# Row factors from squares of the turned input, x in four half slabs, and block sums on GpSimd

## The chip, the cores and the metric

The kernel runs on one core of a Trainium2 chip. The metric is the device time of one execution in microseconds. The times given are the median of three runs and, where a profile is read, the one execution that the hardware profiler recorded.

## The reference, cut to what matters

Two layers of a sandwich-normalised mixer over 512 positions of width 2048, with 256 memory tokens:

```python
def rmsnorm(x, g):
    y = x * lax.rsqrt(jnp.mean(x * x, axis=-1, keepdims=True) + EPS)
    return y * g

for l in range(2):
    h = rmsnorm(x, pre_norm_g[l])                 # x: 512 x 2048
    z = h @ w_in[l]                               # 2048 x 4928
    q_lat, kv_lat, k_pe, gb, gc, xin, q_mem, gate = split_cols(z)
    a_out = mla_attention(...)                    # 8 heads, low-rank q and kv, rotary part
    c_out = short_gated_conv(gb, gc, xin, conv_w[l])
    mem_n = rmsnorm(mem, mem_norm_g[l])           # mem: 256 x 2048
    m_out = memory_attention(q_mem, mem_n, w_mk[l], w_mv[l])   # 4 heads over 256 tokens
    y = concatenate([a_out, c_out, m_out]) * silu(gate)
    x = x + rmsnorm(y @ w_o[l], post_norm_g[l])
```

Everything is float32. The kernel gets x and mem also in turned form (the model width on the partitions), laid out by the host.

## The kernel before, in words

Every float32 product is made as three products of a high and a low part (`mm3`: high by high, low by high or high by low, L253 to L255). ScalarE casts a tile to its high part and VectorE subtracts to get the low part. For weights this is `Program.prep` (L177 and L178) on tiles of 128 x 1024, read by a ring of eight raw tiles (`wr`), with three high (`wh`) and three low (`wl`) tiles. For operands on the left it is `split_to` (L258, L259).

The two large projections use a Strassen form: seven products P1 to P7 of half blocks. Their left operands are A11, A12, A22 and the block sums S1 to S4 (`LEFT`, L357). The weight sums are made on the way in, with accumulating DMAs from the GpSimd queue (`more`, L154). `HEAD`, `STEADY` and others (L400) give the order of the passes. A pass has four steps c = 0 to 3, and a step is 12 matmuls of 512 columns.

`Program.run` goes through a list of steps. For each it issues loads ahead on SP's queue, prepares weights two units ahead, emits the step's work, and then lets put-off work (`pr.defer`) go out as far as the step's `room` covers its cost. `pr.until` and `pr.settle` force it. TensorE, SP and GpSimd keep the order in which the program emits. ScalarE and VectorE keep it up to `first.close`; behind that a scheduler orders them.

Layer 0 starts with the memory products: eight pairs of steps, `keys(kp)` (24 matmuls of 256 columns into four PSUM banks) and `values(kp)` (12 of 512 into two). mem's turned blocks are scaled by a gain column and split (L183, L184). Beside them stand the row factors of x and mem. `row_factors` (L564) loads rows of 128 x 2048, squares them on ScalarE with a running sum (L573), and takes the power -1/2 on GpSimd (L575, L576). `factor_row` (L579) spreads a factor column, turns it on TensorE (L588) and copies it out (L589), so that it can multiply turned data. `turned_load` and `turned_scale` (L591, L595) load x turned in blocks of 128 tokens and multiply by gain and factor row (L598). `left_half` splits A11 and A12.

After the memory steps the kernel runs P1 and P2 of group 0, P1 and P2 of group 1, and then P5 of group 0, the first pass to need a block sum. Tokens 256 to 511 are loaded and scaled during P1 and P2 of group 0 and P1 of group 1. `right_half` and `combine` (L383 to L398) put off the block sums, all on VectorE (L386), with their splits, once per block of 128 tokens:

```python
put_off(nc.vector.tensor_tensor, a22, a22, a21, op=ALU.subtract)
split("S1", a22)
put_off(nc.vector.scalar_tensor_tensor, a22, a22, -1.0, a11, op0=ALU.mult, op1=ALU.subtract)
split("S2", a22)
```

At the end of `values(7)` and `keys(7)` the memory keys and values are scaled, split and written to DRAM (`Kmd`, `Vmd`, L735), to be read back for the attention. Layer 1 does the memory steps again with its own gain and weights, between the transposes of the new x (`transpose_rows`, L601).

Of the kernel before, what the change touches and what calls it, by code (L numbers as in the profile page):

```python
# [12 lines left out]
P = 128  # L13
# [50 lines left out]
class Unit:  # L64
# [6 lines left out]
    def __init__(self, key, loads=None, more=None, sums=(), then=(), place=None, alloc=None, gain=None):  # L71
        self.key = key
        self.loads = loads or {}
        self.more = more
        self.sums, self.then = sums, then
        self.place = place
        self.alloc = alloc
        self.gain = gain


class Program:
# [36 lines left out]
    def run(self):  # L118
# [39 lines left out]
        def prep(upto):  # L158
            while at["prep"] < min(upto, len(seq)):
# [16 lines left out]
                if u.gain is None:  # L176
                    nc.scalar.copy(hi[:, :n], src)  # L177
                    nc.vector.tensor_tensor(lo[:, :n], src, hi[:, :n].bitcast(F32), op=ALU.subtract)  # L178
                else:
                    gains = u.gain()  # L180
                    for k, g in enumerate(gains):
                        h = slice(k * (n // len(gains)), (k + 1) * (n // len(gains)))
                        nc.scalar.activation(hi[:, h], src[:, h], AF.Copy, scale=g)  # L183
                        nc.vector.scalar_tensor_tensor(lo[:, h], src[:, h], g, hi[:, h].bitcast(F32),  # L184
                                                       op0=ALU.mult, op1=ALU.subtract)
                for a, b in u.then:
# [22 lines left out]
def encoder(tc, x, xt, mem, memt, positions, columns, w_in, q_norm_g, w_uq, kv_norm_g, w_ukv,  # L209
# [62 lines left out]
    def setup():  # L272
        ident = scrap("ident", P)
        make_identity(nc, ident)
        identr = const.tile([P, P], F32R, name="identr")
        nc.vector.tensor_copy(identr, ident)
        mhalf = const.tile([P, 4], F32, name="mhalf")
# [105 lines left out]
    def combine(left, p, a11, a12, a21, a22):  # L383
# [14 lines left out]
        split("S3", a21)  # L398

# [164 lines left out]
    def row_factors(key, src, t, dst):  # L564

        def load():
            G[key, t] = slab("rows")
            nc.sync.dma_start(G[key, t], src[t * P:(t + 1) * P, :])

        def factor():  # L570
            rows = G.pop((key, t))
            ssq = small()
            nc.scalar.activation(rows, rows, AF.Square, accum_out=ssq)  # L573
            ms = small(1, "ms")
            nc.gpsimd.tensor_scalar(ms, ssq, 1.0 / D, EPS, op0=ALU.mult, op1=ALU.add)  # L575
            nc.gpsimd.tensor_tensor(dst[:, t:t + 1], ms, G["mhalf"][:, :1], op=ALU.pow)  # L576
        return load, factor

    def factor_row(name, ts):  # L579

        src = G[name]
        dst = scrap("row", len(ts) * P)
        G[name + "_row"] = dst.rearrange("p (t c) -> p t c", c=P)
        ps = bank("rps")
        for k, t in enumerate(ts):
            wide = scrap("wide", P)
            nc.vector.tensor_copy(wide, src[:, t:t + 1].broadcast_to([P, P]))
            nc.tensor.transpose(ps[:, k * P:(k + 1) * P], wide, G["ident"])  # L588
        nc.vector.tensor_copy(dst, ps[:, :len(ts) * P])  # L589

    def turned_load(t):  # L591
        G[f"hT{t}"] = slab("hT").rearrange("p (k c) -> p k c", c=P)
        nc.sync.dma_start(G[f"hT{t}"].rearrange("p k c -> p (k c)"), xt[t])

    def turned_scale(t, h):  # L595
        hT, r = G[f"hT{t}"], G["rx_row"][:, t % 2, :]
        for k in range(8 * h, 8 * h + 8):
            nc.vector.scalar_tensor_tensor(hT[:, k, :], hT[:, k, :], G["g1_0"][:, k:k + 1], r,  # L598
                                           op0=ALU.mult, op1=ALU.mult)
# [30 lines left out]
    def projection(l):  # L630
# [33 lines left out]
        def own_lat():  # L664
# [7 lines left out]
            group(L, (l, 0), 512, block((O_GC, O_XI), 512), slot_of("gc", "xi"), HEAD, fin_u, by_two=l == 0),  # L672
# [12 lines left out]
    def mem_steps(l):  # L685

        def unit(name, w, kp):
            return Unit((name, l, kp), {(name, l, kp): [w[kp * 256:(kp + 1) * 256, :].rearrange("(a p) c -> p a c", p=P)]})

        def turned(q):  # L690
            def place():
                if q % 2 == 0:
                    G.setdefault("mT", []).append((slab("mH", F32R), slab("mL", F32R)))
                return tuple(t[:, (q % 2) * 1024:(q % 2 + 1) * 1024] for t in G["mT"][q // 2])
            return Unit(("mT", l, q), {("mT", l, q): [memt[:, 4 * q:4 * q + 4, :]]}, alloc=place,
                        gain=lambda: [G[f"gm_{l}"][:, 4 * q + a:4 * q + a + 1] for a in range(4)])

        def keys(kp):
            def f(*ops):
# [5 lines left out]
                for i in range(4):  # L705
                    for j in range(2):
                        mm3(G["mk"][i][:, :MT], (kh[:, j, i * P:(i + 1) * P], kl[:, j, i * P:(i + 1) * P]),
                            mem_kt(2 * kp + j), kp == 0 and j == 0, kp == 7 and j == 1)
                if kp == 7:
                    km = G["Km"] = slab("Km", F32R).rearrange("p (s i c) -> p s i c", s=2, i=4)  # L710
                    for i in range(4):
                        ks = scrap("ks", MT)
                        nc.vector.tensor_tensor(ks, G["mk"][i][:, :MT], G["rm_row"].rearrange("p t c -> p (t c)"), op=ALU.mult)
                        split_to(km[:, 0, i, :], km[:, 1, i, :], ks)
            return f

        def values(kp):
            def f(wv):
# [5 lines left out]
                if kp < 7:  # L724
                    return
                vm = G["Vm"] = slab("Vm", F32R).rearrange("p (s t c) -> p s t c", s=2, t=2)
                for t in range(2):
                    r = G["rm"][:, t:t + 1]
                    nc.scalar.activation(vm[:, 0, t, :], G["mv"][t], AF.Copy, scale=r)
                    nc.vector.scalar_tensor_tensor(vm[:, 1, t, :], G["mv"][t], r, vm[:, 0, t, :].bitcast(F32),  # L730
                                                   op0=ALU.mult, op1=ALU.subtract)
                G.pop("mT")
                for n in ("Km", "Vm"):
                    d = G[n + "d"] = dram.tile([P, D], F32, name=f"{n}d{l}")
                    nc.gpsimd.dma_start(d, G.pop(n).rearrange("p a b c -> p (a b c)").bitcast(F32))  # L735
            return f
        return [s for kp in range(8) for s in ((keys(kp), [turned(kp // 2)] * (kp % 2 == 0) + [unit("mk", w_mk[l], kp)], 0.8),
                                               (values(kp), [unit("mv", w_mv[l], kp)], 0.8))]

# [320 lines left out]
    def mixer(l, C, gates, pair2, tail):  # L1060
# [13 lines left out]
        for pair in range(4):  # L1074
# [3 lines left out]
            if pair == 2:  # L1078
                nxt.update(pair2)
            for k, v in nxt.items():  # L1080
# [133 lines left out]
    def warm(n):  # L1214

        ps = bank("warm")
        for k in range(n):
            nc.tensor.transpose(ps[:, (k % 4) * P:(k % 4 + 1) * P], G["ident"], G["ident"])
# [21 lines left out]
    add(pr.begin_loads(5))  # L1240
    add(lambda: warm(30))
    G["src"], G["dst"] = x[0], None
    for l in range(depth):
        G["left"] = L = Left(True)
# [5 lines left out]
        turn = [lambda l=l, t=t: transpose_rows(l, t, G[f"hs{t}"]) for t in range(NT)]  # L1250
        ms = mem_steps(l)
        if l == 0:
            add(use)
            G.update(rx=const.tile([P, NT], F32, name="rx"), rm=const.tile([P, 2], F32, name="rm"))
            xr = [row_factors("x", x[0], t, G["rx"]) for t in range(NT)]
            mr = [row_factors("mem", mem[0], t, G["rm"]) for t in range(2)]
            scale = [[lambda t=t, h=h: turned_scale(t, h) for h in range(2)] for t in range(NT)]
            load = [lambda t=t: turned_load(t) for t in range(NT)]
            left = [[lambda t=t, h=h: left_half(t, (h,)) for h in range(2)] for t in range(2)]
# [149 lines left out]
```

## Time and profile before

| | |
|---|---|
| median of 3 runs | 1521.41 us (1520.81 to 1522.31) |
| profiled execution | 1524.05 us |
| its span, first to last instruction | 1522.3 us |
| mean granted TensorE clock | 0.989 |
| TensorE busy | 1484.2 us (98%) |
| VectorE (DVE) busy | 1095.7 us (72%) |
| ScalarE (ACT) busy | 864.1 us (57%) |
| GpSimd (POOL) busy | 256.4 us (17%), most of it DMA issues |

How to read the profile: a row of an order of time has start, duration, engine, line of the kernel, operation, tile written and tiles read, and in brackets the idle time in front and what ended it. A row of a group has the count, then busy time and mean duration, then idle time in front and what ended it. A row of waits has who waited for whom, the total in us, how often, and the longest. A row of a stretch has the busy time of PE, PEld, DVE, ACT and POOL with instruction counts, then the granted clock, the busy share of the DMA engines and GB/s. PE is TensorE's matmul, PEld its weight load. "Landing" is the end of a DMA.

### The profile page before, as it was taken

The numbers are of one execution on the slowest core, as the hardware profiler recorded it, in microseconds if no ns is written. First come the engines' busy times: TensorE is split into PE (matmuls) and PEld (weight loads), VectorE is DVE, ScalarE is ACT, GpSimd is POOL, SyncE is SP. The second block draws the span as 40 slices with busy tenths as digits, with TensorE's granted clock in tenths as the row PEclk, the third lists the DMA queues.
The fourth block names the chain that finished last, engine by engine and source line by source line (L and its number), as shares of the span: only waits on it lengthen the run. The fifth ranks groups of instructions, "written<-read, shape, count | busy, mean of one in ns | idle before, by whom it ended". The sixth has DMA issues, their size and how long they took to land.

```text
span 1522.3 us, 20025 instructions
## 1 busy us (share of the span) xinstructions
PE 1484.2 (98%) x7494; PEld 1273.7 (84%) x7494; DVE 1095.7 (72%) x1503; ACT 864.1 (57%) x1312; POOL 256.4 (17%) x249
## 2 busy tenths in 40 slices
PE   8897999999999999999999999999999999999997
PEld 8776888899888888887888888888998888888886
DVE  5888867656766768778798856776576586698687
ACT  5554443445557768654687533444454587686443
POOL 0022221212310000140220233020313000003211
PEclk9997999999999999999999999999999999999999
DMA  9996997879891111495887999797979521027945
GB/s 371 343 295 117 239 212 189 171 171 223 190 242 53 56 42 49 112 183 182 242 284 222 245 216 231 192 184 174 182 204 220 177 69 44 28 84 137 249 124 181
DMA packets 143746, 271.39 MB, mean 178 GB/s; under 512 B 17312, under 2 KB 40096, under 8 KB 140320
## 3 DMA queue, kind: packets, MB, share of 16 engines
q0 software_dynamic: 51968, 113.00, 38.9%
q1 hardware_dynamic: 91536, 157.06, 31.1%
q8 instruction: 59, 0.97, 0.3%
q14 instruction: 39, 0.32, 0.1%
q10 hardware_dynamic: 144, 0.05, 0.0%
HBM read 257.49 MB, written 12.58 MB: 177 GB/s over the span
## 4 chain that ended last, share of the span: by engine, by line
PE 83%; DVE 5%; issue 3%; ACT 3%; DMA 2%; POOL 2%; POOLq 0%; DVEq 0%; SPq 0%; ACTq 0%
PE P L254 20%; PE P L255 20%; PE P L253 20%; PE ptp L1000 2%; POOL wr L137 2%; PE tps L751 2%; DVE wl L178 2%; DMA wr<-in_w_o_dram 1%; PE o L254 1%; PE o L255 1%; PE o L253 1%; PE sc L253 1%; PE sc L254 1%; PE sc L255 1%; PE sc L980 1%
## 5 line engine op out<-in xcount | busy, mean ns | idle before, releaser
L178 DVE TENSOR_TENSOR wl<-wr,wh 128x1024 fp32r<-128x1024 f32 (+1 forms) x432 | 515.4, 1198 | 294.5 <-ACT wh L177 285.7
L177 ACT CAST wh<-wr 128x1024 fp32r<-128x1024 f32 (+1 forms) x432 | 444.1, 1032 | 481.3 <-PE P L255 383.6
L253 PE MATMUL P<-wh,S 128*128 128x512 f32 (+1 forms) x896 | 346.9, 387 | 9.0 <-ACT S L258 8.6
L255 PE MATMUL P<-wh,S 128*128 128x512 f32 (+1 forms) x896 | 345.1, 385 | 2.9 <-DVE S L259 2.8
L254 PE MATMUL P<-wl,S 128*128 128x512 f32 (+1 forms) x896 | 345.3, 385 | 1.4 <-DVE wl L178 1.4
L253 PE MATMUL P<-wh,A 128*128 128x512 f32 (+1 forms) x656 | 252.6, 385 | 0.0
L254 PE MATMUL P<-wl,A 128*128 128x512 f32 (+1 forms) x656 | 251.8, 384 | 0.8 <-DVE wl L178 0.8
L255 PE MATMUL P<-wh,A 128*128 128x512 f32 (+1 forms) x656 | 251.4, 383 | 0.0
L137 POOL DMA_DIRECT2D wr<-in_w_in_dram x136 | 164.1, 1207 | 461.3 <-DVE wl L178 279.1
L253 PEld LDWEIGHTS P<-wh,S 128*128 128x128 f32 x896 | 169.0, 189 | 40.2 <-ACT S L258 9.7
L255 PEld LDWEIGHTS P<-wh,S 128*128 128x128 f32 x896 | 169.0, 189 | 34.3 <-DVE S L259 4.0
L254 PEld LDWEIGHTS P<-wl,S 128*128 128x128 f32 x896 | 169.1, 189 | 32.3 <-DVE wl L178 2.4
L254 PEld LDWEIGHTS P<-wl,A 128*128 128x128 f32 x656 | 123.2, 188 | 22.6 <-DVE wl L178 1.2
L255 PEld LDWEIGHTS P<-wh,A 128*128 128x128 f32 x656 | 123.1, 188 | 22.2
L253 PEld LDWEIGHTS P<-wh,A 128*128 128x128 f32 x656 | 123.1, 188 | 21.8 <-ACT og L489 0.2
L137 POOL DMA_DIRECT2D wr<-in_w_o_dram x40 | 48.6, 1214 | 545.9 <-DVE wl L178 530.7
L986 ACT ACTIVATE P<-sc,nm 128x512 f32<-128x512 f32 (+1 forms) x96 | 59.9, 624 | 31.2 <-DVE nm L983 31.2
L989 ACT ACTIVATE P<-P,rec 128x512 f32<-128x512 f32 (+1 forms) x96 | 63.2, 661 | 6.6 <-DVE rec L988 6.6
L983 DVE TENSOR_REDUCE nm<-sc 128x1 f32<-128x512 f32 (+1 forms) x96 | 57.2, 596 | 10.5 <-PE sc L981 6.1
L259 DVE TENSOR_TENSOR PT<-ptp,PT 128x512 fp32r<-128x512 f32 (+1 forms) x96 | 54.9, 595 | 10.0 <-ACT PT L258 9.6
L258 ACT CAST PT<-ptp 128x512 fp32r<-128x512 f32 (+1 forms) x96 | 46.4, 522 | 6.3 <-DVE S L259 3.2
L1000 PE MATMUL ptp<-identr,P 128*128 128x128 f32 x320 | 46.4, 274 | 0.7 <-ACT P L986 0.7
(274 smaller groups left out, 2150.1 us busy)
## 6 DMA issues: line engine op xcount, KB each, us to landing
wr<-in_w_in_dram SPq DMA_DIRECT2D x128, 512.0 KB, 5.2
wr<-in_w_in_dram POOLq DMA_DIRECT2D x112, 512.0 KB, 7.3
wr<-in_w_o_dram SPq DMA_DIRECT2D x48, 512.0 KB, 3.9
wr<-in_w_o_dram POOLq DMA_DIRECT2D x40, 512.0 KB, 7.4
wr<-in_w_in_dram SPq DMA_DIRECT2D x32, 416.0 KB, 3.4
wr<-in_w_in_dram POOLq DMA_DIRECT2D x24, 416.0 KB, 6.0
wr<-in_w_mk_dram SPq DMA_DIRECT2D x16, 512.0 KB, 6.8
wr<-in_w_mv_dram SPq DMA_DIRECT2D x16, 512.0 KB, 6.6
```

Of the source, the lines that this page charges most:

```text
L137: engine.dma_start(dst, src, **kw)
L177: nc.scalar.copy(hi[:, :n], src)
L178: nc.vector.tensor_tensor(lo[:, :n], src, hi[:, :n].bitcast(F32), op=ALU.subtract)
L253: nc.tensor.matmul(ps, ah, bh, start=first, stop=False, **kw)
L254: nc.tensor.matmul(ps, ah, bl, start=False, stop=False, **kw)
L255: nc.tensor.matmul(ps, al, bh, start=False, stop=last, **kw)
L258: nc.scalar.copy(hi, src)
L259: nc.vector.tensor_tensor(lo, src, hi.bitcast(F32), op=ALU.subtract)
L983: nc.vector.tensor_reduce(nmax, ps, axis=AX.X, op=ALU.max, negate=True)
L986: nc.scalar.activation(pt, ps, AF.Exp, bias=nmax, accum_out=tot)
L989: nc.scalar.activation(pt, pt, AF.Copy, scale=rec)
L1000: nc.tensor.transpose(ps[:, k * P:(k + 1) * P], pt[:, k * P:(k + 1) * P], G["ident"])
```

## The change

x comes only turned, in four slabs `X[h][g]` (256 tokens by half the width). Its squares (ScalarE, one instruction of 2048 columns a slab) are folded by GpSimd to 256 columns; the sum over partitions is made by a product with a tile of ones, which leaves the factors as a column. mem's squares and their sums are made by GpSimd from the raw tiles that carry mem to the split. The first gain multiplies X on ScalarE (`turned_gain`), the factor row on VectorE (`turned_scale`, 1024 columns). In layer 0 the left operands are now kept by halves of the width. The block sums are made by GpSimd (`combine_turned`); S2 takes its sign in the split. rm is applied to the memory values and keys behind P1's first steps, from PSUM, and its row goes to DRAM for layer 1. mem's turned blocks of layer 1 are scaled and split during layer 0's second pair of attention heads, written to DRAM (`mTd`) and read back. mem's units are half as large in layer 0. The warm-up products at the start read a tile of ones, 44 instead of 30.

```diff
-                    nc.scalar.copy(hi[:, :n], src)
-                    nc.vector.tensor_tensor(lo[:, :n], src, hi[:, :n].bitcast(F32), op=ALU.subtract)
+                    for k in range(u.parts):
+                        h = slice(k * n // u.parts, (k + 1) * n // u.parts)
+                        nc.scalar.copy(hi[:, h], src[:, h])
+                        nc.vector.tensor_tensor(lo[:, h], src[:, h], hi[:, h].bitcast(F32), op=ALU.subtract)
...
+                if u.beside:
+                    u.beside(src)
...
+    def combine_turned(left, x):
+        u = slab("sums").rearrange("p (a k c) -> p a k c", a=2, k=4)
...
+        def pool_op(o, a, b, op):
+            pr.defer(0.0, lambda: nc.gpsimd.tensor_tensor(o, a, b, op=op))
+        for p in two:
+            a11, a12, a21, a22 = views(p)
+            pool_op(u[:, p], a22, a21, ALU.subtract)
+        for p in two:
+            split("S1", p, u[:, p])
+        for p in two:
+            pool_op(u[:, p], u[:, p], views(p)[0], ALU.add)
+        for p in two:
+            pr.defer(1.2, lambda p=p: negated("S2", p, u[:, p]))
+        for p in two:
+            pool_op(views(p)[1], views(p)[1], u[:, p], ALU.subtract)
+        for p in two:
+            split("S4", p, views(p)[1])
+        for p in two:
+            pool_op(views(p)[2], views(p)[0], views(p)[2], ALU.subtract)
+        for p in two:
+            split("S3", p, views(p)[2])
+        for p in two:
+            split("A22", p, views(p)[3])
...
-    def row_factors(key, src, t, dst):
...
+    def turned_squares(h, g):
+        sq = slab("sq")
+        nc.scalar.activation(sq, G["X"][h][g].rearrange("p k c -> p (k c)"), AF.Square)
+        add_up(sq, 2048)
+        if g:
+            first = G["sq", h]
+            nc.gpsimd.tensor_tensor(first[:, :256], first[:, :256], sq[:, :256], op=ALU.add)
+        else:
+            G["sq", h] = sq
+    def add_up(t, n):
+        while n > 256:
+            n //= 2
+            nc.gpsimd.tensor_tensor(t[:, :n], t[:, :n], t[:, n:2 * n], op=ALU.add)
+    def mem_squares(kp):
+        def f(src):
...
+            acc, new = t[:, :512], t[:, 512:1024]
+            nc.gpsimd.tensor_tensor(new if kp else acc, src, src, op=ALU.mult)
+            if kp:
+                nc.gpsimd.tensor_tensor(acc, acc, new, op=ALU.add)
+            if kp == 7:
+                add_up(t, 512)
+        return f
+    def factor_split(h):
+        red = scrap("red", dt=F32R)
+        split_to(red[:, :256], red[:, 256:], G.pop(("sq", h))[:, :256])
+        G["red", h] = red
+    def factor_columns(h, ps, dst):
+        red = G.pop(("red", h))
+        for t in range(2):
+            for i in range(2):
+                nc.tensor.matmul(ps[:, t * P:(t + 1) * P], red[:, i * 256 + t * P:i * 256 + (t + 1) * P], G["onesr"],
+                                 start=i == 0, stop=i == 1)
+        ms = small(NT, "ssq4")[:, :2]
+        nc.vector.tensor_scalar(ms, ps[:, :256].rearrange("p (t c) -> p t c", c=P)[:, :, 0], 1.0 / D, EPS,
+                                op0=ALU.mult, op1=ALU.add)
+        nc.gpsimd.tensor_tensor(dst, ms, G["mhalf"][:, :2], op=ALU.pow)
...
+    def turned_gain(h, g, a):
+        X = G["X"][h][g]
+        for k in range(4 * a, 4 * a + 4):
+            nc.scalar.activation(X[:, k, :], X[:, k, :], AF.Copy, scale=G["g1_0"][:, 8 * g + k:8 * g + k + 1])
+    def turned_scale(h, g, p):
+        X = G["X"][h][g][:, 4 * p:4 * p + 4, :]
+        r = G[f"rx{h}"].rearrange("p (o c) -> p o c", o=1).broadcast_to([P, 4, 256])
+        nc.vector.tensor_tensor(X, X, r, op=ALU.mult)
...
+            if pair == 1 and l + 1 < depth:
+                for k, s in enumerate(mem_turned_steps(l + 1)):
+                    nxt.setdefault(2 * k + 1, []).append(s)
...
             beside = {
-                0: [xr[0][0]], 1: [xr[1][0]], 2: [xr[0][1], load[0]], 4: [xr[1][1], load[1]],
...
+                1: [lambda: turned_load(1, 0)], 2: [squares(0, 0)], 3: [lambda: turned_load(1, 1)],
+                4: [squares(0, 1)], 5: [gain(0, 0, 0)], 6: [gain(0, 0, 1)],
+                7: [lambda: factor_split(0), columns_of(0)], 8: [row_of(0)], 9: [gain(0, 1, 0), squares(1, 0)],
+                10: [scaled(0, 0, 0)], 11: [left_part(0, 0, 0), squares(1, 1)], 12: [scaled(0, 0, 1)],
+                13: [left_part(0, 0, 1), gain(0, 1, 1)], 14: [scaled(0, 1, 0), lambda: factor_split(1), columns_of(1)],
+                15: [left_part(0, 1, 0), row_of(1), lambda: factor_split("m")],
             }
...
+            put(a[:1])
+            add(lambda: factor_columns("m", G["mk"][0][:, MT:], G["rm"]))
+            add(scaled(0, 1, 1))
+            add(left_part(0, 1, 1))
+            put(a[1:2])
+            add(lambda: factor_row("rm_row", G["mk"][1][:, MT:], G["rm"]))
+            add(lambda: values_out(0))
...
+            put(a[2:3])
+            add(lambda: keys_out(0))
+            put(a[3:])
+            add(first.close)
+            for g in range(2):
+                for k in range(2):
+                    add(lambda g=g, k=k: pr.defer(0.0, gain(1, 1 - g, k)))
+            for g in (1, 0):
+                for k in range(2):
+                    add(lambda g=g, k=k: pr.defer(1.2, scaled(1, g, k)))
+            add(lambda: pr.defer(0.0, lambda: combine_turned(G["left"], G["X"])))
```

More of the change, by code (lines that the diff above doesn't have):

```diff
@@ L64, with __init__ @@
 class Unit:
-    def __init__(self, key, loads=None, more=None, sums=(), then=(), place=None, alloc=None, gain=None):
+    def __init__(self, key, loads=None, more=None, sums=(), then=(), place=None, alloc=None, gain=None, parts=1,
+                 beside=None):
         self.key = key
@@ L579, in factor_row @@
[L579 to L593, printed above, removed]
@@ L732, in f @@
[L732 to L735, printed above, removed]
+                if kp == 7:
+                    G.pop("mT")
             return f
-        return [s for kp in range(8) for s in ((keys(kp), [turned(kp // 2)] * (kp % 2 == 0) + [unit("mk", w_mk[l], kp)], 0.8),
+        return [s for kp in range(8) for s in ((keys(kp), [turned(kp)] * (l == 0) + [unit("mk", w_mk[l], kp)], 0.8),
@@ L740, in mem_fetch, with mem_reload @@
+    def mem_reload(h):
+        two = slab("mH", F32R), slab("mL", F32R)
+        for i in range(2):
+            nc.gpsimd.dma_start(two[i], G["mTd"][2 * h + i])
+        G.setdefault("mT", []).append(two)
     def mem_fetch():
@@ L1271, in encoder @@
                     add(f)
-            add(first.close)
         else:
```

191 lines of the change are left out of this document (117 added, 74 removed).

## The prediction, made before the changed kernel ran

> **What bounds the kernel now.** I read the page's engine shares first, then the list of what TensorE (PE) waits for, then PE's order of time around those waits, and last the order of time of VectorE (DVE) and GpSimd (POOL).
>
> ```profile
> PE 1484.2 (98%) x7494; PEld 1273.7 (84%) x7494; DVE 1095.7 (72%) x1503; ACT 864.1 (57%) x1312; POOL 256.4 (17%) x249
> ```
> ```profile
> PE P L253 <- ACT S L258: 8.6, 2, 8.4
> PE mk L255 <- DVE wl L178: 3.3, 4, 1.2
> PE rps L588 <- DVE wide L587: 2.9, 1, 2.9
> PE P L255 <- DVE S L259: 2.8, 1, 2.8
> ```
> ```profile
> 100.00:120.00 20.00, 12.68 (x50) 9.31 (x48) 19.96 (x29) 9.87 (x10) 4.76 (x4) 0.83 1.07 254
> ```
>
> PE is busy 98% of the span, so the time can only come from its 38 us of idleness and from slow clock. The list of waits (total us, times, longest) names the block sums first; its longest entries lie before 130 us, as PE's order of time below shows. In the stretch from 100 to 120 us the columns are PE, PEld, DVE, ACT, POOL busy, then granted clock: while PE stands a third of the time and the clock falls to 0.83, DVE is busy 19.96 of 20 us. That is the block sums S1 to S4 of layer 0, all made by DVE just as P5 needs them. PE's order of time gives the places:
>
> ```profile
> 14.95 0.40 PE L253 MATMUL mv<-wh,mH 128*128 128x512 f32 x1
> ...
> 20.57 0.40 PE L253 MATMUL mv<-wh,mH 128*128 128x512 f32 x1
> ...
> 64.86 0.39 PE L253 MATMUL P<-wh,A 128*128 128x512 f32 x1
> 65.09 0.39 PE L254 MATMUL P<-wl,A 128*128 128x512 f32 x1
> ...
> 110.03 0.50 PE L253 MATMUL P<-wh,S 128*128 128x512 f32 x1 [0.16 <-ACT S L258]
> ...
> 124.02 0.79 PE L253 MATMUL P<-wh,S 128*128 128x512 f32 x1 [8.40 <-ACT S L258]
> ...
> 126.36 0.63 PE L254 MATMUL P<-wl,S 128*128 128x512 f32 x1
> 126.79 0.63 PE L255 MATMUL P<-wh,S 128*128 128x512 f32 x1
> ```
>
> A pair of memory steps takes 20.57 - 14.95 = 5.62 us, so eight pairs take 45. A 512-wide matmul takes 0.23 us at full clock (64.86 to 65.09) and 0.43 behind a long stall (126.36 to 126.79). P1 begins at 64.86, P5 at 110.03. P5 loses 0.16 + 2.78 + 8.40 = 11.3 us of idleness and about 20 slow matmuls of 0.2, 4 us: 15.3 together. Without those, its start would be worth 110.0 + 15.3 = **125.3**. The same point in the changed kernel decides the case; I work out two times, to P1 and from P1 to P5.
>
> **The prices.** DVE's and ACT's groups in the first 70 us (busy, mean ns), then ACT's first row, which waits for mem, and three of DVE's weight splits in a row:
>
> ```profile
> L177 ACT CAST wh<-wr 128x1024 fp32r<-128x1024 f32 x19 | 19.3, 1042 | 10.0 <-PE mk L254 6.2 <-PE mv L255 3.7
> L573 ACT ACTIVATE rows<-rows 128x2048 f32<-128x2048 f32 x4 | 7.7, 1913 | 2.8 <-DMA rows<-in_x_dram 2.8
> L183 ACT ACTIVATE mH<-wr,cols 128x256 fp32r<-128x256 f32 x16 | 6.8, 497 | 0.0
> L184 DVE SCALAR_TENSOR_TENSOR mL<-wr,cols,mH 128x256 fp32r<-128x256 f32 x16 | 6.7, 480 | 5.7 <-ACT mH L183 5.7
> ```
> ```profile
> 5.45 1.28 ACT L183 ACT_TABLE_LOAD   x1 [5.45 <-DMA wr<-in_memt_dram]
> ```
> ```profile
> 9.42 3.50 DVE L178 TENSOR_TENSOR wl<-wr,wh 128x1024 fp32r<-128x1024 f32 x3 [0.45 <-ACT wh L177]
> ```
>
> So DVE does 1024 columns in 3.50 / 3 = 1.17 us. GpSimd has no large sum in this trace. Its nearest rows are small:
>
> ```profile
> 0.72 0.20 POOL masks.py:197 MEMSET ident<- 128x128 f32 x1 [0.29 <-POOLq L1391]
> 1.00 0.29 POOL masks.py:199 TENSOR_SCALAR_AFFINE_SELECT ident<-ident 128x128 f32<-128x128 f32 x1
> 1.25 0.10 POOL L278 MEMSET mhalf<- 128x4 f32 x1
> ```
>
> The fill of 128 columns costs 0.10 us over the smallest one, 0.8 ns a column; one that also reads a tile costs 0.19 over it, 1.5 ns. A second input should add what the first did, 0.7: **2.2 ns** a column as an estimate, with 1.5 as the low bound. That is 2.35 us for 1024 columns, 1.23 for 512, 0.66 for 256.
>
> **Do GpSimd and DVE run side by side?** A DVE row, then two GpSimd rows, of which the second starts inside it, and GpSimd's group of such rows:
>
> ```profile
> 786.87 1.28 DVE L1183 SCALAR_TENSOR_TENSOR xr<-og,r,xr 128x1024 f32<-128x1024 f32 x1
> ```
> ```profile
> 771.10 0.55 POOL L265 TENSOR_TENSOR r<-ms,mhalf 128x1 f32<-128x1 f32 x1 [5.11 <-DVE ms L263]
> ...
> 787.13 1.44 POOL L265 TENSOR_TENSOR r<-ms,mhalf 128x1 f32<-128x1 f32 x1 [2.91 <-DVE ms L263]
> ```
> ```profile
> L265 POOL TENSOR_TENSOR r<-ms,mhalf 128x1 f32<-128x1 f32 x12 | 11.3, 944 | 52.7 <-DVE ms L263 32.1 <-DVE tot L1123 16.6 <-ACT wh L177 3.9
> ```
>
> The same one-column power takes 0.55 us at 771, but 1.44 when it starts inside a DVE instruction with two SBUF inputs. It ends at 788.57, 0.4 us after that instruction's end at 788.15: it has stood for nearly all of it. The group's mean of 944 ns says that this is common. So GpSimd does not read while DVE streams two inputs. Whether DVE waits in turn for a long GpSimd sum no row shows, since these powers read one column. I take it that it does: one way is seen, and a shared path explains it both ways.
>
> The Trainium skill, "SBUF — State Buffer", section "Who interferes with whom", states that rule: a DVE instruction with two SBUF inputs and a GpSimd instruction that reads SBUF exclude each other, and the second waits for all of the first. The trace agrees for GpSimd as the one that waits. By the rule the time is that of the sum in line below; if only what the rows show held, it would be that of the sum side by side.
>
> **The change up to P1.** GpSimd now squares and sums mem (a product and a sum of 512 columns per pair of blocks) and adds up the squares of x, in program order, and PE needs the second pair of row factors before the last values step. Up to there GpSimd has 13 instructions of 512 (16.0 us), four folds 1024 + 512 + 256 (17.0) and two sums of 256 (1.3): 34.3. DVE has 17 weight splits (19.9), 16 mem splits (6.7), five products with the factor row or splits of x (5.9): 32.5, all with two SBUF inputs. If they exclude each other, that is 67 us in line. It starts when the first mem piece lands; half as large as now, it comes before 5.45. I take 4.5. So 71.5, then the last values step, 2.7, and a row copy: **P1 at 75**, 10 us late. Side by side, ACT would set the time: 17 casts (17.3), mem scalings 6.8, squares of x 7.7, 32 gains of 256 columns (13.6 at the mem scaling's price), two casts of x: 47.5, against PE's 45. From 4.5, with the factor's path and the last step behind, that is P1 at 56.5.
>
> Queued behind a late sum: ACT's split of the factor sums and with it ACT's next weight casts; on SP the w_mv loads, since a raw tile is now returned by GpSimd too. What goes away hides nothing: 6 MB of row loads and six row squares, and the 2.9 us wait for rm's row (`rps`). A smaller first piece, its weights split in two halves and an earlier table load bring the first matmul forward; that is inside both P1 times, which start from ACT and DVE.
>
> **From P1 to P5.** New in both cases is rm's row inside P1: its transposes stand on PE after two steps (24 matmuls, 5.5 us), but on DVE the copy that feeds them stands behind eight two-input instructions (five products with the factor row, a split of x, two weight splits), 9.4 us, and a few small ones, 1.0. PE waits 4.9 us, and by the slow rows above some eight matmuls at 0.2 are lost, 1.6. Sixteen steps of twelve matmuls are 43.7 us; with this, **P5 at P1 + 50** if nothing else ends later.
>
> The block sums are eight GpSimd instructions of 1024, behind Km's write in the GpSimd queue, which waits for Km:
>
> ```profile
> 59.43 0.42 DVE L713 TENSOR_TENSOR ks<-mk,row 128x256 f32<-128x256 f32 x1
> ...
> 64.01 0.43 DVE L259 TENSOR_TENSOR Km<-ks,Km 128x256 fp32r<-128x256 f32 x1 [0.47 <-ACT Km L258]
> ```
>
> Km takes 5 us, so they start at P1 + 10.4 + 8.6 = 19 (row, Vm, one split, Km). From there DVE has 12 weight splits, 10 splits of sums and two evictions, 27 us, before P5's first weights, and GpSimd 18.8: in line, **P5 at P1 + 65**. ACT's casts of S stand ahead of its weight casts, and the accumulating loads stand between the sums on GpSimd, so both wait with them. Side by side the chain ends at about P1 + 50 as well, with nothing to spare.
>
> In line: 75 + 65 = 140 against 125.3, **+14.7**. Side by side: 56.5 + 50 = 106.5, **-18.8**.
>
> **Layer 1.** mem's scaling and split move from the start of layer 1 into layer 0's attention; four units of 1.7 us on ACT and on DVE, eight writes, four reads.
>
> ```profile
> 796.41 0.38 PE L253 MATMUL mk<-mH,wh 128*128 128x256 f32 x1 [0.77 <-ACT wh L177]
> 798.14 0.38 PE L255 MATMUL mk<-mH,wl 128*128 128x256 f32 x1 [1.22 <-DVE wl L178]
> ```
> ```profile
> 400.00:600.00 200.00, 198.22 (x1143) 171.95 (x1143) 133.07 (x232) 136.16 (x265) 12.00 (x11) 1.00 0.40 101
> ```
>
> The two waits, 2.0 us, can go with it. In the attention ACT and DVE are idle a third of the time and DMA is at 0.40, which covers the moved work; if the three split buffers come back late from their writes, it costs at most a unit, 2 us. Bounds -2 to +2; I take -2, since the waits stand where the work was.
>
> **The numbers.** In line: +14.7 - 2 = +12.7. Some of DVE's work reads PSUM and can overlap, 2 us: **+11**. The profiled execution took 1524.05 us with a span of 1522.3, 2.6 over the median of 1521.41; I add the difference to the median: **1532**. Own range 1524 to 1543. A measurement can tell 0.2%, 3 us, from no change.
>
> **Rivals.** (1) *Side by side*: GpSimd only starts late, DVE is never held. For it: no DVE row is stretched by a GpSimd one. Against it: the rows above. -18.8 - 2 gives **1501**. It decides once less than about 60% of GpSimd's time is added to DVE's. (2) *Cheaper sums*: in line, but at 1.5 ns a column. GpSimd's 34.3 become 23.5 and its 18.8 become 12.9; P1 at 64 and P5 at P1 + 59 give -2.3 - 2 = -4; with latencies between dependent sums, **1519**. (3) *Late tiles*: in line, and a raw tile that GpSimd returns late starves PE of weights once as well.
>
> ```profile
> wr<-in_w_mv_dram SPq DMA_DIRECT2D x8, 512.0 KB, 9.1
> ```
>
> One such load, 9.1 us from issue to landing in the first 70 us, gives 1532 + 9 = **1541**.
>
> **Chances.** In line 0.50, side by side 0.27, cheaper sums 0.14 (faster 0.06, same 0.07, slower 0.01), late tiles 0.09. Faster 0.33, same 0.07, slower 0.60. The range runs from 1502 to 1543, which leaves out the lower half of side by side (0.13) and of late tiles the upper part (0.04).
>
> **What would show it.** In line: DVE's weight splits well over 1.22 us or apart from each other while GpSimd sums run, GpSimd sums of 1024 near or over 2.35 us, P1 after 70 us, P5 after 130. Side by side: P1 before 60. In either, a PE wait of some 5 us for rm's row in P1, and layer 1 starting without its 0.77 and 1.22. The prediction is wrong if splits keep 1.17 us beside the sums, or if P5 starts before 120.

## The result, and the profile after

The changed kernel takes 1540.25 us (median of four runs, 1538.57 to 1542.82), beside 1521.86 us for the kernel before (four runs, 1520.81 to 1524.82). The ratio is 1.0119, with a 95% interval from 1.0099 to 1.0140: slower by 18.4 us. The profiled execution took 1542.82 us with a span of 1541.0, 18.7 more than the span before. In the changed kernel's profile the line numbers are others: `mm3` is L260 to L262, the weight cast and split L182 and L183, the block sums L429, the folds of the squares L634, mem's squares L642 and L644.

The engine shares of the page say where the added work went. GpSimd has 73 us more than before; TensorE's own share is lower because the span grew:

```profile
PE 1493.9 (97%) x7518; PEld 1282.6 (83%) x7518; DVE 1119.1 (73%) x1444; ACT 872.4 (57%) x1341; POOL 329.8 (21%) x292
```

TensorE's waits in the first 170 us (us in total, times, longest) no longer name the block sums' casts. They name the weight splits on VectorE:

```profile
PE P L261 <- DVE wl L183: 13.0, 2, 8.1
PE fps L659 <- DVE red L266: 4.8, 2, 3.3
PE mk L673 <- DVE wide L672: 4.4, 1, 4.4
PE mk L262 <- DVE wl L183: 3.7, 3, 1.8
PE mv L261 <- DVE wl L183: 2.1, 1, 2.1
```

TensorE's order of time gives the places: the start of P1, the wait for rm's row, the two waits in P1 and P2 for a weight split, the start of P5.

```profile
77.14 0.48 PE L260 MATMUL P<-wh,A 128*128 128x512 f32 x1
...
87.68 0.69 PE L673 MATMUL mk<-identr,wide 128*128 128x128 f32 x2 [4.38 <-DVE wide L672]
...
102.89 0.80 PE L261 MATMUL P<-wl,A 128*128 128x512 f32 x1 [4.95 <-DVE wl L183]
...
132.59 0.80 PE L261 MATMUL P<-wl,A 128*128 128x512 f32 x1 [8.10 <-DVE wl L183]
...
146.16 0.39 PE L260 MATMUL P<-wh,S 128*128 128x512 f32 x1
```

P1 begins at 77.14 (64.86 before) and P5 at 146.16, against the 125.3 that the start before was worth without its later waits: 20.9 us lost. Behind P5 the changed kernel is shorter: 1541.0 - 146.16 = 1394.8 us, against 1522.3 - 125.3 = 1397.0. That is 20.9 - 2.2 = 18.7, the whole difference of the spans. Of the 69.0 us from P1 to P5, 16 steps at 2.73 us are 43.7 and the three waits are 17.4. Of the rest, 7.9 us, some 1 us is six small products of 128 columns for rm's factor and row, and some 7 us is matmuls that take longer than 0.23 us, behind those waits: between 120 and 140 us the granted clock (the number before the DMA share) is 0.74.

```profile
120.00:140.00 20.00, 11.90 (x40) 9.32 (x39) 20.00 (x10) 9.26 (x11) 12.54 (x7) 0.74 0.88 217
```

In that stretch VectorE counts as busy for 20.00 us with only ten instructions. VectorE's and GpSimd's orders of time show what it did. The first fence has VectorE's rows, at the start of the block sums and at the place of the 8.10 us wait, and the second has GpSimd's:

```profile
96.73 8.37 DVE L183 TENSOR_TENSOR wl<-wr,wh 128x1024 fp32r<-128x1024 f32 x3 [0.52 <-ACT wh L182]
...
120.65 10.76 DVE L313 CAST posf<-posi 128x4 f32<-128x4 int32 x1
131.32 1.21 DVE L183 TENSOR_TENSOR wl<-wr,wh 128x1024 fp32r<-128x1024 f32 x1
```
```profile
97.06 4.68 POOL L429 TENSOR_TENSOR sums<-X,X 128x1024 f32<-128x1024 f32 x2
106.32 2.38 POOL L429 TENSOR_TENSOR sums<-sums,X 128x1024 f32<-128x1024 f32 x1 [4.58 <-DVE S L266]
...
120.37 5.18 POOL L429 TENSOR_TENSOR X<-X,sums 128x1024 f32<-128x1024 f32 x2
...
126.05 5.32 POOL L429 TENSOR_TENSOR X<-X,X 128x1024 f32<-128x1024 f32 x2
```

Three splits that take 3.50 us before take 8.37: they are longer by the two sums beside them (it is the first split that stands, for 6.10 us). And a cast of four columns counts 10.76 us: it begins while the four last sums begin, and ends at 131.41, when the last of them ends (131.37). The split that TensorE waits for stands behind it. Before P1 the same is seen in smaller pieces. GpSimd alone does 512 columns in 1.04 us, and its folds of 1024, 512 and 256 columns take 6.50 while two splits beside them take 5.67 in place of 2.35. Here the engines take turns: the first split ends at 29.51 us, the first fold at 31.77, the second split at 32.86, the second fold at 33.99.

```profile
3.64 1.04 POOL L642 TENSOR_TENSOR sqm<-wr 128x512 f32<-128x512 f32 x1 [2.29 <-DMA wr<-in_memt_dram]
...
28.38 6.50 POOL L634 TENSOR_TENSOR sq<-sq 128x1024 f32<-128x1024 f32 x3
```
```profile
27.19 5.67 DVE L183 TENSOR_TENSOR wl<-wr,wh 128x1024 fp32r<-128x1024 f32 x2
```

### The profile page after: what moved, and what is told of

It reads as the page before. It is cut to its first block, busy times and chain, and to the rows that moved or that the text cites. A ratio compares the mean times of both kernels' runs of the same rounds, so it can differ in the third digit from the quotient of the medians.

```text
span 1541.0 us, 20111 instructions
## 1 busy us (share of the span) xinstructions
PE 1493.9 (97%) x7518; PEld 1282.6 (83%) x7518; DVE 1119.1 (73%) x1444; ACT 872.4 (57%) x1341; POOL 329.8 (21%) x292
## 4 chain that ended last, share of the span: by engine, by line
PE 70%; issue 13%; DVE 8%; ACT 3%; POOL 3%; DMA 2%; POOLq 0%; DVEq 0%; ACTq 0%
PE P L261 18%; PE P L260 18%; PE P L262 18%; DVE wl L183 3%; POOL wr L140 2%; DMA wr<-in_w_in_dram 1%; PE ptp L1109 1%; PE tps L860 1%; PE o L261 1%; PE o L262 1%; PE mk L260 1%; PE o L260 1%; PE mk L261 1%; PE mk L262 1%; DMA wr<-in_w_o_dram 1%
## 5 line engine op out<-in xcount | busy, mean ns | idle before, releaser
L183 DVE TENSOR_TENSOR wl<-wr,wh 128x1024 fp32r<-128x1024 f32 (+2 forms) x433 | 534.3, 1238 | 297.5 <-ACT wh L182 287.2
L182 ACT CAST wh<-wr 128x1024 fp32r<-128x1024 f32 (+2 forms) x433 | 444.5, 1029 | 479.5 <-PE P L262 389.6
L260 PE MATMUL P<-wh,S 128*128 128x512 f32 (+1 forms) x896 | 345.2, 385 | 1.4 <-ACT wh L182 1.4
L262 PE MATMUL P<-wh,S 128*128 128x512 f32 (+1 forms) x896 | 343.2, 383 | 0.0
L260 PE MATMUL P<-wh,A 128*128 128x512 f32 (+1 forms) x656 | 255.2, 389 | 0.0
L262 PE MATMUL P<-wh,A 128*128 128x512 f32 (+1 forms) x656 | 253.9, 387 | 0.0
L260 PEld LDWEIGHTS P<-wh,S 128*128 128x128 f32 x896 | 168.1, 188 | 31.5 <-ACT wh L182 1.8
L262 PEld LDWEIGHTS P<-wh,S 128*128 128x128 f32 x896 | 168.2, 188 | 30.3
L262 PEld LDWEIGHTS P<-wh,A 128*128 128x128 f32 x656 | 124.7, 190 | 22.9
L260 PEld LDWEIGHTS P<-wh,A 128*128 128x128 f32 x656 | 124.8, 190 | 22.3 <-ACT og L540 0.2
```

The costliest lines, as they stand in the source:

```text
L182: nc.scalar.copy(hi[:, h], src[:, h])
L183: nc.vector.tensor_tensor(lo[:, h], src[:, h], hi[:, h].bitcast(F32), op=ALU.subtract)
L260: nc.tensor.matmul(ps, ah, bh, start=first, stop=False, **kw)
L262: nc.tensor.matmul(ps, al, bh, start=False, stop=last, **kw)
```

## The experiments

The theory: GpSimd's two-input sums and VectorE's instructions stand in line, so GpSimd's time is added to VectorE's wherever VectorE is late. The rivals: a chain of dependent sums is late whoever else works; or ScalarE, the transfers or the order of instructions hold the start. Each kernel is the changed one with the edit shown. The kernel before took 1521.3 to 1522.6 us beside them. Where no interval is given, a time is one execution. Six executions of one kernel ranged over almost 5 us, and eleven of the kernel before over 8.6, so such runs are read first by the starts of P1 and P5. Five kernels have the same code up to P1 (the changed one, the two that follow, and the two with fillers); they began it between 75.08 and 77.14 us, so a difference of 2 us at P1 says nothing.

**The cast that stood for 10.76 us, moved to ScalarE.**

```diff
-            nc.vector.tensor_copy(pf, G["posi"])
+            nc.scalar.copy(pf, G["posi"])
```

> The changed kernel, but the cast of the positions (128x4, 10.76 us long in the changed kernel's profile, while four GpSimd sums ran) is made by ScalarE. Theory A, the cast is a separate loss on top of the sums in line: VectorE no longer stands there, P5 starts some 8 us earlier (138 instead of 146), and the time is some 8 us less, near 1532. Theory B, VectorE and GpSimd use one path in line and the cast only decided whose turn it was: the four sums, 9.4 us, are paid between the splits instead, P5 starts within 3 us of 146, and the time stays within 1537 to 1543.

Measured: 1539.33 us, P5 at 145.37, TensorE's wait still 8.24 us. The time went to the next instruction on VectorE, which is a weight split with two inputs:

```profile
118.73 13.04 DVE L183 TENSOR_TENSOR wl<-wr,wh 128x1024 fp32r<-128x1024 f32 x2
```

Two splits take 13.04 us here, 10.7 too many. So the cast was no loss of its own, and its form was not needed for it: a split in its place waits out the same run of GpSimd's sums.

**The block sums on VectorE.**

```diff
-            pr.defer(0.0, lambda: nc.gpsimd.tensor_tensor(o, a, b, op=op))
+            pr.defer(1.2, lambda: nc.vector.tensor_tensor(o, a, b, op=op))
```

> The changed kernel, but the eight block sums of layer 0 are made by VectorE. In line (my theory): 8 x 2.35 = 18.8 us of GpSimd become 8 x 1.17 = 9.4 of VectorE in the same queue, so from P1 to P5 9 us go, and the cast no longer stands behind GpSimd; P5 at 146 - 9 to -14, time 1526 to 1532. Side by side (rival): the sums cost VectorE nothing where they are, and moved they add 9.4 us to it; P5 no earlier than 146, time 1540 to 1550. P1 stays at 77 by both.

Measured: 1519.8 us, 20 less than the changed kernel, a larger gain than was expected. P1 starts at 75.08 and P5 at 126.54, P1 + 51.5:

```profile
75.08 0.48 PE L260 MATMUL P<-wh,A 128*128 128x512 f32 x1
...
126.54 0.39 PE L260 MATMUL P<-wh,S 128*128 128x512 f32 x1
```

Between the two, TensorE waits once, 4.37 us for rm's row. VectorE carries eight sums more, at 1.22 us each, and is still not late. On GpSimd the same sums cost 17.5 us between P1 and P5: the waits of 4.95 and 8.10 and 4.4 us of slow clock behind them.

**GpSimd work that nobody waits for, beside the last kernel's sums:** eight sums of a spare tile, or eight fills of it.

```diff
+        f = slab("filler")
+        nc.gpsimd.memset(f, 0.0)
...
             pr.defer(1.2, lambda: nc.vector.tensor_tensor(o, a, b, op=op))
+            pr.defer(0.0, lambda: nc.gpsimd.tensor_tensor(f[:, :1024], f[:, :1024], f[:, 1024:], op=ALU.add))
```

> Kernel: the one with the block sums on VectorE, and beside each of the eight sums a GpSimd sum of two inputs of 1024 columns on a spare tile that nobody reads. Its time against that kernel's 1519.8 is what eight such GpSimd instructions cost by themselves, since nothing waits for their results. Theory A (GpSimd sums and VectorE's two-input instructions run in line, so GpSimd's time is added where VectorE is the engine that sets the time): 8 x 2.35 = 18.8 us are added to VectorE between P1 and P5, P5 at P1 + 62 to 71, 1533 to 1541. Theory B (in the changed kernel it was the chain of dependent sums, not their time on VectorE's path, that made P5 late): nothing depends on these, P5 stays at P1 + 52, 1519 to 1523.

The other kernel has `nc.gpsimd.memset(f, 0.0)` in the last line:

> The same with eight GpSimd fills of 2048 columns of the spare tile in place of the sums: about as long on GpSimd (some 1.6 us each by 0.8 ns a column), but they read nothing. If only GpSimd instructions that read hold VectorE: P5 at P1 + 52, 1519 to 1523. If any work of GpSimd on the memory holds it: 13 us more on VectorE, some 1528 to 1534.

Measured: 1539.7 us with the sums, 1520.5 with the fills. Eight instructions whose results nobody uses cost 19 us when they read two inputs, and nothing that single executions can show when they only write (1519.8 without either). So the cost needs no chain of dependent sums. But P5 did not start at P1 + 62 or later, as the theory had it: it started at P1 + 53, near the rival's P1 + 52, and the time went behind it. Only two of the eight sums were done by then, and beside these the engines took turns, one instruction each. GpSimd, then VectorE:

```profile
98.40 6.51 POOL L432 TENSOR_TENSOR filler<-filler 128x1024 f32<-128x1024 f32 x2
```
```profile
99.58 3.08 DVE L183 TENSOR_TENSOR wl<-wr,wh 128x1024 fp32r<-128x1024 f32 x1 [0.26 <-ACT wh L182]
102.58 3.42 DVE L431 TENSOR_TENSOR sums<-X,X 128x1024 f32<-128x1024 f32 x1
```

A split and a sum on VectorE take 3.08 and 3.42 us in place of 1.22, and the two GpSimd sums 6.51 in place of 4.7. What came later looks different. GpSimd, VectorE, ScalarE and TensorE:

```profile
116.95 17.48 POOL L432 TENSOR_TENSOR filler<-filler 128x1024 f32<-128x1024 f32 x1
134.38 1.18 POOL L140 DMA_DIRECT2D wr<-in_w_in_dram  x1
```
```profile
132.10 1.27 DVE L506 TENSOR_TENSOR gb<-gb,P 128x512 f32<-128x512 f32 x2
```
```profile
140.34 1.04 ACT L182 CAST wh<-wr 128x1024 fp32r<-128x1024 f32 x1 [12.18 <-DMA wr<-in_w_in_dram]
```
```profile
141.44 0.79 PE L260 MATMUL P<-wh,S 128*128 128x512 f32 x1 [6.21 <-ACT wh L182]
```

Here VectorE had the upper hand. From 115 to 132 us its instructions with two SBUF inputs follow each other without a gap, and one GpSimd sum stands for 17.48 us. It ends 2.33 us after 132.10, when VectorE first does something else (an eviction from PSUM). Behind that sum, in GpSimd's queue, stands an accumulating load of weights. It goes out only at 134.38, ScalarE has no weights, and TensorE waits. So the line is real in both directions, but its order is not fixed: beside the first two sums and before P1 of the changed kernel the engines take turns, here one of them keeps the other out for 17 us. What decides between the two no run here shows.

In the kernel with the fills VectorE's two-input instructions keep their 1.22 us beside a fill. The cast of four columns, which reads one input, does not keep its time. A fill, the cast beside it, and the cast in the kernel that has the block sums on VectorE and no filler:

```profile
132.59 2.33 POOL L432 MEMSET filler<- 128x2048 f32 x1
```
```profile
133.65 1.40 DVE L313 CAST posf<-posi 128x4 f32<-128x4 int32 x1
```
```profile
128.97 0.17 DVE L313 CAST posf<-posi 128x4 f32<-128x4 int32 x1
```

The cast ends at 135.05, 0.13 us after the fill (134.92), and takes 1.40 us in place of 0.17. So what stands beside a fill depends on the instruction, though this one cost the kernel nothing that shows.

The Trainium skill, "SBUF — State Buffer", section "Who interferes with whom", says that a VectorE instruction with two SBUF inputs contends with a GpSimd instruction that reads SBUF but not with one that only writes it. The two filler kernels agree, 1539.7 against 1520.5 us. It also says, of VectorE's two-port modes, that whoever issues first has the shared pair of ports for the whole instruction; the traces here show turns of one instruction, and also runs of 10.7 and 17 us.

**Fewer sums before P1.** mem's squares are made from two of its eight pairs of blocks:

```diff
         def f(src):
+            if 0 < kp < 7:
+                return
```

> The changed kernel, but the squares of mem are summed over 2 of its 8 pairs of blocks only (the memory factors are then not mem's): 12 GpSimd instructions of 512 columns fewer before P1, 1.1 to 1.3 us each by the changed kernel's profile, 14 us. In line: P1 comes some 10 to 14 us earlier, at 63 to 67, and the time falls by as much, to 1526 to 1530. Rival, ScalarE sets the time up to P1 (47.5 us of work, and it stands in front of the weight casts): P1 moves by less than 4 us, time over 1535.

Measured: 1534.7 us, P1 at 72.45. Some 12 us of GpSimd's work gone, 4.7 gained (2.6 to 4.7 against the five kernels above), half of the least that was expected; neither forecast holds. Work of one engine waits for another here: GpSimd's last folds 4.39 us for ScalarE's squares, and ScalarE's casts of x 2.8 and 3.3 us for VectorE's products with the row. But the same waits are in the changed kernel (4.05, 5.01 and 3.27), so they do not show where the missing microseconds went; that stays open.

**The row factors from rows again**, with everything else as changed: the loads of rows and ScalarE's squares with a running sum come back, and GpSimd's squares and folds go.

```diff
+    def row_squares(key, t, dst):
+        rows = G.pop((key, t))
+        ssq = small()
+        nc.scalar.activation(rows, rows, AF.Square, accum_out=ssq)
...
-                1: [lambda: turned_load(1, 0)], 2: [squares(0, 0)], 3: [lambda: turned_load(1, 1)],
...
+                0: [load("x", 0)], 1: [load("x", 1)], 2: [lambda: turned_load(1, 0), factor("x", 0)],
+                3: [lambda: turned_load(1, 1)], 4: [factor("x", 1)], 5: [gain(0, 0, 0), load("x", 2)],
```

> The changed kernel, but all row factors are taken from rows again (x and mem loaded as rows, squared on ScalarE with a running sum), so GpSimd has only powers of one column before P1; half slabs, early block sums and all else stay. In line: 34 us of GpSimd leave the path before P1, and P1 comes at 56 to 62 instead of 77; from P1 to P5 nothing changes, P5 at about 127; time 1521 to 1526. Rival, the 6 MB of rows or ScalarE hold it: P1 after 68, time over 1531.

Measured: 1533.6 us, P1 at 72.56. Freed from GpSimd's sums VectorE is hardly busy, but P1 is no earlier than in the last kernel, as the rival had it. In the stretch from 20 to 40 us (PE, PEld, DVE, ACT, POOL busy, clock, DMA share, GB/s) the DMA engines are busy throughout, a share of 1.03:

```profile
20.00:40.00 20.00, 15.87 (x81) 13.88 (x80) 5.75 (x7) 16.36 (x30) 1.48 (x4) 0.83 1.03 405
```

ScalarE waits there 7.07 us for the first rows, with its weight casts behind, and TensorE 3.47 for those. With the block sums on VectorE, the cast on ScalarE and a shorter start added to this kernel:

> The row factors from rows again (no GpSimd sums before P1), the block sums on VectorE, the position cast on ScalarE and 24 products ahead. The kernel with rows and GpSimd block sums began P1 at 72.6 with ScalarE at 10 of 10 from 30 to 50 us. If ScalarE and the transfers hold it there: P1 at 70 to 73, P5 at P1 + 51, 1515 to 1519. If it was the late start: P1 at 66 to 69, 1511 to 1514.

Measured: 1521.1 us. P1 at 72.62 again, P5 at P1 + 51.0. The wait for rows is 8.82 us on ScalarE and 6.88 on TensorE. So rows have a price of their own, the wait for their transfer: the kernel below that has neither rows nor GpSimd sums begins P1 6 us earlier.

**A shorter start** (from here on every kernel has the block sums on VectorE and the position cast on ScalarE):

```diff
-    add(lambda: warm(44))
+    add(lambda: warm(24))
```

> The block sums on VectorE, the position cast on ScalarE, and 24 products of ones ahead of the first step in place of 44. If the 44 products stand ahead of the first step (they end at 10.4 us, the weights are there near 7): first matmul near 7 to 8, 2 to 3 us earlier, and if the start carries through to P1, 1516 to 1518. If GpSimd and VectorE set P1 whatever the start: P1 stays at 75, 1519 to 1520.

Measured: 1518.5 us. The first matmul comes at 6.37 in place of 10.49, as expected, but P1 only at 74.36, against 75.08 to 77.14 with 44 products: four microseconds at the start are worth 0.7 to 2.8 at P1. What comes behind the start sets the rest.

**The factor of x's second half made in P1**, in place of the last memory steps:

```diff
-                14: [scaled(0, 1, 0), lambda: factor_split(1), columns_of(1)],
-                15: [left_part(0, 1, 0), row_of(1), lambda: factor_split("m")],
+                14: [scaled(0, 1, 0)],
+                15: [left_part(0, 1, 0), lambda: factor_split("m")],
...
             add(lambda: keys_out(0))
+            add(lambda: factor_split(1))
+            add(columns_of(1))
+            add(row_of(1))
```

> As the last one, and the factor of the second half of x (split, ones products, row) made after P1's third step in place of the last values steps. TensorE loses its wait of 2.0 us for the factor sums ahead of P1 and some small products. If that wait was on the path: P1 2 to 4 us earlier, 1513 to 1516. If the row then comes too late for the scaled second half and its block sums, P5 gets a wait of 3 to 8 us and it is 1518 to 1524.

Measured: 1521.3 us. P1 comes 3.7 us earlier, at 70.62, but TensorE then waits 4.96 and 1.31 us for the moved factor in P1, and P5 starts at 127.89, 2.2 later than without the move. The wait was on the path, and moved with the work.

**All sums and products of the factors on VectorE**, the folds of x's squares one step behind the squares:

```diff
-            nc.gpsimd.tensor_tensor(t[:, :n], t[:, :n], t[:, n:2 * n], op=ALU.add)
+            nc.vector.tensor_tensor(t[:, :n], t[:, :n], t[:, n:2 * n], op=ALU.add)
...
-            nc.gpsimd.tensor_tensor(new if kp else acc, src, src, op=ALU.mult)
+            nc.vector.tensor_tensor(new if kp else acc, src, src, op=ALU.mult)
```

> As the kernel with the short start and the block sums on VectorE, and every other sum and product of the row factors taken from GpSimd to VectorE as well; the folds of x's squares stand one step behind the squares. Theory A (up to P1 too GpSimd and VectorE run in line, so a sum costs the pair 2.0 to 2.35 ns a column on GpSimd but 1.1 on VectorE): GpSimd's 34 us before P1 become some 17 on VectorE, 32.5 + 17 = 50 in line in place of 67, P1 at 62 to 68 in place of 74.4, 1507 to 1513. Theory B (ScalarE's order and the waits between the engines hold P1, not the sums): P1 at 72 to 76, 1516 to 1521.

Measured: 1513.5 us, P1 at 66.47 and P5 at 117.65. That is 7.9 us earlier at P1 than with the sums on GpSimd, although VectorE now has some 20 us more to do (eight products and seven sums of 512 columns at 0.69 us, four folds at 2.40). From 40 to 60 us the two kernels look alike in VectorE's busy time (the third number: with the sums on GpSimd, then without), but not in what was done, 12 instructions in one and 26 in the other:

```profile
40.00:60.00 20.00, 15.56 (x84) 13.21 (x83) 17.85 (x12) 12.04 (x19) 15.47 (x11) 0.93 0.58 172
```
```profile
40.00:60.00 20.00, 14.78 (x88) 13.27 (x87) 19.73 (x26) 18.26 (x33) 0.00 (x0) 0.90 0.59 178
```

So up to P1 too the two engines run in line, and a sum of 1024 columns costs the pair 2.38 us on GpSimd but 1.22 on VectorE. (The folds also came one step later; what that alone is worth no run shows.) The same kernel timed in five rounds:

> The kernel without GpSimd sums once more, timed in five rounds on one chip with the kernel before: 1513.5 was one execution. Expected 1513 to 1514.5, 0.994 to 0.996 of the kernel before.

Measured: 1512.09 us (six runs, 1510.65 to 1514.45), the kernel before beside it 1522.54. The ratio is 0.9931, interval 0.9914 to 0.9947, a little better than expected, with P1 at 66.16 and P5 at 117.75.

**rm's row one step later**, its copies earlier on VectorE, in that kernel:

```diff
             add(scaled(0, 1, 1))
+            add(lambda: G.update(rm_wide=widened(G["rm"])))
             add(left_part(0, 1, 1))
-            put(a[1:2])
-            add(lambda: factor_row("rm_row", G["mk"][1][:, MT:], G["rm"]))
+            put(a[1:3])
+            add(lambda: factor_row("rm_row", G["mk"][1][:, MT:], G["rm"], G["rm_wide"]))
...
-            put(a[2:3])
```

> The kernel without GpSimd sums (1513.5), and in it the row of rm: its two widened columns are copied on VectorE ahead of the split and the products that stood before them, and its transposes stand on TensorE one step (2.73 us) later. There TensorE waited 4.30 us, with about 1.6 of slow clock behind it. If that wait was on the path that sets the end: 4 to 6 us off, 1507.5 to 1509.5. If what VectorE has to do up to P5 (19.7 of 20 us busy from 40 to 60, 20.0 from 100 to 120) sets the end anyway: another wait comes in P1 or P2, 1511 to 1514.

Measured: 1511.42 us (six runs, 1509.9 to 1514.67), ratio to the kernel before 0.9927, interval 0.9912 to 0.9943. It is not told apart from the last one. The wait for the row is gone, and another stands in P1, for a weight cast. ScalarE has it behind four casts of the keys, which wait 3.37, 1.40, 0.83 and 0.83 us for VectorE's products:

```profile
84.42 0.49 PE L260 MATMUL P<-wh,A 128*128 128x512 f32 x1 [3.26 <-ACT wh L182]
```

P5 starts at 118.78, no earlier than 117.65. The wait was moved, and VectorE's work stands behind the new one too.

## Why the prediction was right or wrong

The direction and the mechanism were right, and the time was 8 us short: +11 was predicted, +18.4 measured. By its own terms, in the spans:

- **GpSimd's prices** held: 2.35 us estimated for 1024 columns, 2.38 measured where it runs alone; 1.23 for 512, 1.04 measured. That the first came out within 0.03 us is in part luck: the estimate was drawn from rows of 128 columns and from a guess at the second input.
- **P1 at 75**: it started at 77.14, 2.1 later, which is no more than the five kernels with the same code differ by; one of them began at 75.08. The sum had the line of the two engines right. It did not count that work of the one also waits for ScalarE (GpSimd's last folds, for example, begin 4.05 us after it was free), nor that 44 products ahead of the first step bring the first matmul to 10.49, later than the 9.44 before, which by the kernel with 24 is worth 0.7 to 2.8 us at P1. And fewer sums before P1 gave half of what the line alone promised. So that the total came out is in part luck.
- **rm's row**: a wait of 4.9 us was worked out, 4.38 measured.
- **P5 at P1 + 65**: it was P1 + 69.0. This is the term that was most mis-sized. VectorE's standing was foreseen well: 4.9 us in the three splits, 2.0 in one and 10.6 in the cast, 17.5 together, against 18.8. But the sum went along VectorE alone. VectorE also waits 4.0 us for ScalarE's casts of weights (2.82, 0.37, 0.84), and TensorE runs slowly behind each of its waits, some 7 us in all, of which the prediction counted 1.6, for rm's row only.
- **Layer 1, -2**: its two waits are gone, and what follows P5 is 2.2 us shorter. In the other kernels, the one with filler sums apart, what follows P5 is 1.2 to 6.7 us shorter than the 1397.0, so the size is not settled to 2 us.
- **Overlap through PSUM, -2**: nothing of it is seen. VectorE's two evictions between the start of the sums and P5, 114.91 to 116.18, fall where no GpSimd sum runs. This term should not have been taken off.

The sum is then 2.1 at P1, 4.0 from P1 to P5, 2 for the overlap and -0.2 for layer 1, 7.9 us on the predicted 10.7: the 18.7 of the spans, within rounding.

Of the rivals, *side by side* is refuted by the rows in which VectorE stands (8.37, 10.76 and, with the cast moved, 13.04 us) and by the block sums on VectorE, which by that rival would have put P5 at 146 or later and put it at 126.54. Its P1 at 56.5 no kernel here came near: the one with rows, nearly free of GpSimd sums, does not get below 72.5, where it waits for the rows, and the ones with no sums on GpSimd and no rows begin at 65.5 to 66.5. *Cheaper sums* was wrong on the price. *Late tiles* came near the time (1541), but not by its mechanism: in the changed kernel the late weights are splits that stand on VectorE. The late load that it spoke of is what the filler sums show.

What the prediction did not weigh at all is where to do the sums. If GpSimd and VectorE are in line, then GpSimd is the dearer of the two for the same sum by a factor of two (2.38 against 1.22 us), and the change with its sums on VectorE and a shorter start beats the kernel before by 10 us.

## What to carry to other kernels

Work with two SBUF inputs that is handed to GpSimd beside a busy VectorE is not offloaded. Where VectorE sets the time, it takes its own time from VectorE, twice what VectorE itself would have needed, so count both engines as one and look for sums on GpSimd wherever a split on VectorE shows a multiple of its usual time. A fill that only writes cost VectorE's two-input instructions nothing there, but held a cast of one input. And before such work is put on GpSimd, look at what its queue issues: a sum that was kept out for 17 us held back the weight load behind it.

## What was not expected of the hardware

The two engines do not always change over between two instructions. Before P1 and beside the first two filler sums they did. But four GpSimd sums with DMA issues between them kept a cast of 128 x 4 on VectorE for 10.76 us, where it takes 0.17 us with the sums on VectorE, and when the cast was moved away a split stood 10.7 us in its place. Conversely a run of VectorE instructions with two SBUF inputs kept one GpSimd sum of 2.35 us for 17.48 us, until the first VectorE instruction that read PSUM. And a fill, which reads nothing, left two-input splits at 1.22 us but that same cast took 1.40 beside one.
